# Token sums in four parts behind the evacuations of a chunk, and no modulation steps in that chunk

## The chip, the cores and the metric

The kernel runs on one core of one Trainium2 chip. The metric is device time in microseconds (us) of one execution. TensorE (PE) multiplies, VectorE (DVE), ScalarE (ACT) and GpSimd (POOL) do the element-wise work, and SyncE (SP) issues most of the transfers. Each engine takes its instructions from its own queue, in order.

## The reference

What is computed is a two-layer transformer on 512 latent tokens and 256 context tokens with a width of 1024. In each layer a half feed-forward step (SwiGLU, inner width 2816), a token mixer (neighbourhood attention in layer 0, windowed attention in layer 1) and a second half feed-forward step follow each other. Each of them is modulated by vectors that a product of the conditioning vector with a large matrix gives (`wmod`), and is closed by a layer norm:

```python
def swiglu(u, w_in, w_out):
    a, v = jnp.split(u @ w_in, 2, axis=-1)
    return (jax.nn.silu(a) * v) @ w_out

def ffn_sublayer(h, shift, scale, gate, w_in, w_out, g, b):
    y = swiglu(modulate(h, shift, scale), w_in, w_out)
    return layer_norm(ALPHA * h + FFN_RES * gate * y, g, b)
```

All of it is float32.

## The kernel before

**Layout.** Activations lie feature-major: eight tiles of 128 features by 768 tokens. A float32 value is kept as the sum of a high and a low part in TensorE's fp32r format, so `uh[d]` and `ul[d]` together are the modulated input of a step, and each product is three matmuls (lines L146, L147, L148: high by high, low by high, high by low). `z[d]` is the residual.

**Four feed-forward calls.** They are named 0a, 0b, 1a and 1b (layer, first or second half step) and all run through `ffn`. The inner width is cut into 11 chunks of two 128-row tiles. A *plain* chunk computes its a and v products for group a (512 tokens; 256 in 1b) and for group b (256 tokens), in the order (a, tile 0), (b, 0), (a, 1), (b, 1). One such step is an `av`: 48 matmuls, then DVE multiplies v by silu(a) in place (`pv`, L451), ACT copies the high part (`gh`, L452) and DVE subtracts to get the low part (`gl`, L453). After the four of them 16 *downs* follow (`pd`, eight output tiles for each group), and DVE adds each to the residual (`z`, L427). The downs of such a chunk, and the products of the chunks after it, take their PSUM banks from a ring of six.

**Seven products.** The first chunks are plain: three in 0a (chunks 0, 1, 2), two in 0b, 1a and 1b (chunks 0, 1). This number is `s0`. From chunk `s0` to chunk 8 each tile is computed by a Strassen-Winograd scheme on halves of the tokens and quarters of the weights: seven products p0 to p6 in place of eight (`seven`), whose evacuations DVE and ACT do (L565, L569). A tile's seven are followed by the next, and between the two of one chunk the downs of the chunk before run. POOL makes the sums of weight quarters (`S`, L536) and low parts of weights (`wl`, L104).

**Token sums.** The scheme needs sums of the token halves: `x1`, `x2` and `x3`, each for four pairs of feature tiles j. For one j these are 5 DVE operations and 3 POOL operations (L485), 3 ACT copies to the high parts and 3 DVE subtractions to the low parts (`T`, L507), all on 128x384 elements (128x256 in 1b). `sums()` writes them down at the start of chunk `s0 - 1`, with eight transfers per call that save the halves to be overwritten later. `fourth()` makes the fourth sum in place after that chunk (two POOL, one ACT and two DVE operations per j, L517 to L521); only product 6 needs it. Products 3, 2 and 5 need x1, x2 and x3.

**Modulation steps.** The modulation vectors of later steps are computed in the background on DVE. One *step* is a multiply-and-reduce `jk` of 128x512 elements (L198) followed by a 128x1 read of the accumulator. Its weights come in 256 KB loads that SP issues (L195) into two buffers `wt` and a spare tile `zspare`, so that at most three loads are out at a time. A load serves two steps where the vectors of the latent and the context tokens are both wanted ("two streams"), one step otherwise. `tick()` issues steps by a counter: `weight` (L601) gives each chunk its share and `each` (L602) scales the shares so that all steps of the call fit. 0a, 0b and 1a have such steps, 1b has none.

**What sets the order.** The order written in the code is a wish. A scheduler plays all instructions through a timeline and puts each engine's queue in the order in which they would start there; on the chip a queue is then worked off strictly in order. `behind(x, y)` (L308) adds a constraint: x stays behind y on the same engine. `last[0]` is the latest multiply, accumulate or product evacuation. Steps are issued `behind` it. In the kernel before, the token sums have no such constraint, so the scheduler puts them as early as their inputs exist.

Of the kernel before, what the change touches and what calls it, by code (L numbers as in the profile page):

```python
# [8 lines left out]
F32 = mybir.dt.float32  # L9
F32R = mybir.dt.float32r  # L10
# [3 lines left out]
ALU = mybir.AluOpType  # L14
# [4 lines left out]
P = 128  # L19
# [7 lines left out]
NCH = NF // 2  # L27
# [11 lines left out]
def hybrid_kernel(ctx: ExitStack, tc: tile.TileContext, h0, cc, crow, wmod, wmodt, bmod, lnp, wst,  # L39
                  rpbp, nmask, sinks, ropec, rmat, ident, wmask, out):  # L40
    nc = tc.nc
# [5 lines left out]
    dp = ctx.enter_context(tc.tile_pool(name="dp", bufs=1, space=DRAM))  # L47
# [5 lines left out]
    def t2(nm, tag="t2"):  # L53
        return tp.tile([P, 512], F32, tag=tag, name=nm, bufs={"t2": 6, "ln": 2, "sl": 2}[tag])
# [25 lines left out]
    uh = [rp.tile([P, NT], F32R, name=f"uh{d}") for d in range(DT)]  # L80
    ul = [rp.tile([P, NT], F32R, name=f"ul{d}") for d in range(DT)]
# [104 lines left out]
    bg, last, last_exp, wtq = [], [None], [None], [0]  # L186
# [244 lines left out]
    def ffn(nm, groups, gt, mid, post, units=(), opened={}, head=None, apart=None):  # L431
# [40 lines left out]
        n2 = nb * P  # L472

        def half(t, h):

            return t[:, 0:nb * 256].rearrange("p (a s b) -> p s a b", s=2, b=P)[:, h]

        def as_half(t):
            return t.rearrange("p (a b) -> p a b", b=P)

        ts = [[[None, None] for _ in range(4)] for _ in range(3)]

        def op(eng, out, a, b, o):
            a, b = [half(y[0], y[1]).bitcast(F32) if isinstance(y, tuple) else as_half(y) for y in (a, b)]
            eng.tensor_tensor(out=as_half(out), in0=a, in1=b, op=o)  # L485

        def sums():


            saved = dp.tile([2, 4, P, n2], F32, name=f"sv{nm}")  # L490
            for j in range(4):
                for x, t in enumerate((uh, ul)):
                    nc.sync.dma_start(saved[x, j].rearrange("p (a b) -> p a b", b=P), half(t[j], 1).bitcast(F32))
                x1, x2, x3 = [t2(f"x{nm}_{j}_{i}")[:, 0:n2] for i in range(3)]
                k = j + 4
                op(nc.vector, x1, (uh[j], 1), (uh[j], 0), ALU.subtract)
                op(nc.vector, x1, x1, (ul[j], 1), ALU.add)
                op(nc.vector, x1, x1, (ul[j], 0), ALU.subtract)
                op(nc.gpsimd, x3, (uh[k], 1), (uh[j], 1), ALU.subtract)
                op(nc.gpsimd, x3, x3, (ul[k], 1), ALU.add)  # L500
                op(nc.gpsimd, x3, x3, (ul[j], 1), ALU.subtract)
                op(nc.vector, x2, (uh[k], 1), x1, ALU.subtract)
                op(nc.vector, x2, x2, (ul[k], 1), ALU.add)
                for i, x in enumerate((x1, x2, x3)):
                    hi, lo = [ph["T"].tile([P, 384], F32R, tag=f"T{i}{j}{y}", name=f"T{nm}_{i}_{j}{y}", bufs=1)[:, 0:n2] for y in "hl"]
                    nc.scalar.copy(hi, x)
                    nc.vector.tensor_tensor(out=lo, in0=x, in1=hi.bitcast(F32), op=ALU.subtract)  # L507
                    ts[i][j] = [as_half(hi), as_half(lo)]
            return saved

        def fourth():

# [83 lines left out]
        if mid is not None:  # L596
            mid()
        gts.append(gt())
        late_downs = []
        s0 = 3 if opened else 2  # L600
        weight = [0] + [1.6] * (s0 - 1) + [1.0] * (NCH - 2 - s0)  # L601
        each = sum(n + 1 for n, _ in bg) / (sum(weight) - 0.1)  # L602
        for ci in list(range(NCH)) + [("r", NCH - 2)]:
            r = isinstance(ci, tuple)
            if not r and 0 < ci < NCH - 2:
                phase("T")
                pace[0] = each * weight[ci] / (4 if ci < s0 else 14)
                if ci == s0 - 1:
                    saved = sums()
            if not r and s0 <= ci < NCH - 2:  # L610
                gs = [[gp.tile([P, NT], F32R, tag="gs", name=f"g{x}{nm}_{ci}_{i}", bufs=6) for x in "hl"] for i in range(2)]

# [29 lines left out]
            def avs(*todo):  # L642
                for g, i in todo:
                    av(w[i], f"{cn}_{i}", g, *gs[i], opened.get((i, g)) if ci == 0 else None, 4 if late else 0)
                    if not r and 0 < ci < s0:
                        tick()

            def dn(g):
                down(w[2], cn, gs, g, not r and 0 < ci < NCH - 2)

            a, b = groups
# [654 lines left out]
```

## Time and profile before

| | |
|---|---|
| median of three runs | 2864.95 us (2863.02 to 2868.26) |
| the profiled execution | 2872.14 us, its span 2870.4 us |
| mean granted TensorE clock | 0.977 |
| PE busy | 2723.7 us (95% of the span) |
| DVE busy | 1857.1 us (65%) |
| ACT busy | 1211.9 us (42%) |
| POOL busy | 1687.2 us (59%) |
| modulation steps in all | 416, of 0.68 us each |
| idle time of DVE before steps, waiting for a load | 62.1 us (`wt`) and 12.3 us (`zspare`) |

The profile is of one execution. Tile names in it have lost their numbers: `pd0b` is any down of call 0b, `x0b` any token sum of it, `p60a` a product 6 of 0a. A row of the view by windows gives, for a stretch of time, each engine's busy time and number of instructions, and then the clock that TensorE was granted as a share of full speed. A row of waits gives an engine's operation, what it waited for, the total in us, the number of waits and the longest.

In the times of the span, chunk 0 of 0a ends near 130 us and its chunk-2 downs run from 195.6 to 212.6; the seven products of 0a run to 490. 0b's chunk 0 is near 1086 to 1122, its chunk-1 downs are at 1140.9 to 1169.2, its products run to 1480. 1a's chunk 0 is near 1640, its chunk-1 downs are at 1700.4 to 1717.4, its products run to 2040. 1b's chunks 0 and 1 lie at 2500 to 2550.

### The profile page before, as it was taken

The numbers are of one execution on the slowest core, as the hardware profiler recorded it, in microseconds if no ns is written. First come the engines' busy times: TensorE is split into PE (matmuls) and PEld (weight loads), VectorE is DVE, ScalarE is ACT, GpSimd is POOL, SyncE is SP. The second block draws the span as 40 slices with busy tenths as digits, with TensorE's granted clock in tenths as the row PEclk, the third lists the DMA queues.
The fourth block names the chain that finished last, engine by engine and source line by source line (L and its number), as shares of the span: only waits on it lengthen the run. The fifth ranks groups of instructions, "written<-read, shape, count | busy, mean of one in ns | idle before, by whom it ended". The sixth has DMA issues, their size and how long they took to land.

```text
span 2870.4 us, 48094 instructions
## 1 busy us (share of the span) xinstructions
PE 2723.7 (95%) x17122; PEld 2444.4 (85%) x17122; DVE 1857.1 (65%) x4122; ACT 1211.9 (42%) x2496; POOL 1687.2 (59%) x1488
## 2 busy tenths in 40 slices
PE   8999999999999979999999899999998999899997
PEld 5789999888888878899998789899886777788897
DVE  3597776385545687766554886666457667787745
ACT  4223433266455453333433424333336655444443
POOL 4547674475433565776744777666456545577763
PEclk9999999999999989999999999999999999999998
DMA  8465556232211222445452345656431111235462
GB/s 299 126 189 161 157 141 162 78 85 83 65 56 51 65 60 88 114 125 136 118 139 74 93 119 140 175 153 181 133 95 46 51 38 45 60 89 129 122 180 67
DMA packets 285872, 322.16 MB, mean 112 GB/s; under 512 B 28480, under 2 KB 174016, under 8 KB 284608
## 3 DMA queue, kind: packets, MB, share of 16 engines
q1 hardware_dynamic: 269792, 290.63, 34.2%
q0 software_dynamic: 15552, 28.32, 5.9%
q8 instruction: 135, 2.21, 0.3%
q14 instruction: 105, 0.86, 0.1%
q10 hardware_dynamic: 288, 0.14, 0.0%
HBM read 311.14 MB, written 12.25 MB: 113 GB/s over the span
## 4 chain that ended last, share of the span: by engine, by line
PE 73%; DVE 14%; DMA 5%; issue 3%; ACT 2%; POOL 2%; SPq 0%; DVEq 0%; POOLq 0%; ACTq 0%
DMA wt<-in_wmodt_dram 2%; PE pd0b L146 2%; PE pd0b L147 2%; PE pd0b L148 2%; DVE jk L198 2%; PE pd1a L146 2%; PE pd1a L147 2%; PE pd1a L148 2%; DMA wr<-in_wst_dram 1%; DVE z L427 1%; PE pd0a L146 1%; PE wo L753 1%; PE pd0a L147 1%; PE pd0a L148 1%; PE o L753 1%
## 5 line engine op out<-in xcount | busy, mean ns | idle before, releaser
L104 POOL TENSOR_TENSOR wl<-wr,wh 128x512 fp32r<-128x512 f32 x308 | 406.4, 1335 | 293.2 <-ACT wh L102 261.5
L104 POOL TENSOR_TENSOR wl_s<-S,wh_s 128x512 fp32r<-128x512 f32 x202 | 269.2, 1368 | 52.8 <-ACT wh_s L102 49.5
L102 ACT CAST wh<-wr 128x512 fp32r<-128x512 f32 x308 | 186.8, 620 | 225.7 <-DMA wr<-in_wst_dram 54.5
L102 ACT CAST wh_s<-S 128x512 fp32r<-128x512 f32 x216 | 131.6, 620 | 335.7 <-POOL S L536 79.6
L536 POOL TENSOR_TENSOR S<-wr,wr 128x512 f32<-128x512 f32 x108 | 147.6, 1367 | 180.2 <-DMA wr<-in_wst_dram 172.0
L198 DVE CUSTOM_DVE_ANT_0 jk<-wt,cb 128x512 f32<-128x512 f32 x278 | 185.2, 680 | 63.7 <-DMA wt<-in_wmodt_dram 62.1
L104 POOL TENSOR_TENSOR wl_a<-wr,wh_a 128x512 fp32r<-128x512 f32 x120 | 159.6, 1383 | 26.7 <-ACT wh_a L102 17.5
L102 ACT CAST wh_a<-wr 128x512 fp32r<-128x512 f32 x162 | 100.5, 621 | 134.1 <-PE pd1b L147 18.1
L427 DVE SCALAR_TENSOR_TENSOR z<-pd0b,gt,z 128x256 f32<-128x256 f32 (+1 forms) x176 | 102.3, 602 | 62.7 <-PE pd0b L148 62.5
L427 DVE SCALAR_TENSOR_TENSOR z<-pd1a,gt,z 128x512 f32<-128x512 f32 (+1 forms) x168 | 99.0, 620 | 39.2 <-PE pd1a L148 39.0
L427 DVE SCALAR_TENSOR_TENSOR z<-pd0a,gt,z 128x512 f32<-128x512 f32 (+1 forms) x168 | 98.1, 620 | 31.9 <-PE pd0a L148 31.5
L760 POOL TENSOR_SCALAR p<-p,l 128x512 f32<-128x512 f32 x64 | 44.5, 696 | 118.9 <-DVE l L858 110.5
L305 POOL TENSOR_SCALAR z<-z,ag_None,ab_None 128x256 f32<-128x256 f32 (+1 forms) x78 | 73.0, 942 | 47.6 <-DVE uh L291 38.7
L198 DVE CUSTOM_DVE_ANT_0 jk<-zspare,cb 128x512 f32<-128x512 f32 x138 | 92.5, 680 | 12.3 <-DMA zspare<-in_wmodt_dram 12.3
L760 POOL TENSOR_SCALAR pw<-pw,l 128x512 f32<-128x512 f32 (+1 forms) x64 | 41.0, 642 | 68.2 <-DVE l L1047 27.7
L536 POOL TENSOR_TENSOR S<-S,wr 128x512 f32<-128x512 f32 x54 | 77.2, 1429 | 2.9 <-DVE x1b L519 0.4
L536 POOL TENSOR_TENSOR S<-wr,S 128x512 f32<-128x512 f32 x54 | 76.4, 1414 | 3.1 <-PE pv0a L148 0.5
L857 ACT ACTIVATE p<-s,m 128x512 f32<-128x512 f32 x64 | 44.0, 688 | 76.2 <-DVE m L855 71.2
L287 ACT ACTIVATE ufl<-z,bi_None,sc_None 128x256 f32<-128x256 f32 (+1 forms) x86 | 54.5, 654 | 37.2 <-DVE z L406 36.9
L427 DVE SCALAR_TENSOR_TENSOR z<-pd1b,gt,z 128x512 f32<-128x512 f32 (+1 forms) x98 | 56.3, 609 | 13.1 <-PE pd1b L148 13.1
L292 DVE TENSOR_TENSOR ul<-ufl,uh 128x256 fp32r<-128x256 f32 (+1 forms) x88 | 61.7, 711 | 1.0 <-ACT uh L289 0.7
L146 PE MATMUL vn<-wh,uh 128*128 128x256 f32 x192 | 54.9, 286 | 2.4 <-DVE nl L716 1.8
(1445 smaller groups left out, 10757.9 us busy)
## 6 DMA issues: line engine op xcount, KB each, us to landing
wr<-in_wst_dram SPq DMA_DIRECT2D x524, 256.0 KB
wt<-in_wmodt_dram SPq DMA_DIRECT2D x160, 256.0 KB
zspare<-in_wmodt_dram SPq DMA_DIRECT2D x80, 256.0 KB
wr_0b<-in_wst_dram SPq DMA_DIRECT2D x42, 256.0 KB
wr_1b<-in_wst_dram SPq DMA_DIRECT2D x42, 256.0 KB
wr_2b<-in_wst_dram SPq DMA_DIRECT2D x42, 256.0 KB
wr_3b<-in_wst_dram SPq DMA_DIRECT2D x42, 256.0 KB
wm<-in_wmod_dram SPq DMA_DIRECT2D x8, 1024.0 KB
```

The source lines that it names most:

```text
L102: nc.scalar.copy(hi[:], src[:])
L104: eng.tensor_tensor(out=lo[:], in0=src[:], in1=hi[:].bitcast(F32), op=ALU.subtract)
L146: nc.tensor.matmul(ps, a[0], b[0], start=first, stop=False)
L147: nc.tensor.matmul(ps, a[0], b[1], start=False, stop=False)
L148: nc.tensor.matmul(ps, a[1], b[0], start=False, stop=last)
L198: x = nc.vector.tensor_tensor_reduce(out=junk[:], in0=w[:], in1=cb[st], scale=1.0, scalar=0.0, op0=ALU.mult, op1=ALU.add, accum_out=acc[:, ...
L292: return hi, nc.vector.tensor_tensor(out=lo, in0=uv, in1=uo.bitcast(F32), op=ALU.subtract)
L305: nc.gpsimd.tensor_scalar(out=zs, in0=zs, scalar1=prm[2][:, d:d + 1], scalar2=prm[3][:, d:d + 1], op0=ALU.mult, op1=ALU.add)
L427: last[0] = nc.vector.scalar_tensor_tensor(out=zt(d, c0, c1), in0=pd, scalar=gt[:, d, st:st + 1], in1=zt(d, c0, c1), op0=ALU.mult, op1=ALU ...
L536: nc.gpsimd.tensor_tensor(out=t[:], in0=a[:], in1=b[:], op=o)
L753: nc.tensor.matmul(po[64 * h:64 * h + 64, :], t[h][0], t[h][1], start=i == 0, stop=i == len(terms) - 1)
L760: nc.gpsimd.tensor_scalar(out=p, in0=p, scalar1=r, scalar2=0.0, op0=ALU.mult, op1=ALU.add)
```

## The change

`sums()` is split. The saving transfers become `save()`, still issued at the start of chunk `s0 - 1`. The rest becomes `sums(j)`, called once behind each of the four `av` steps of that chunk, one j at a time, and each DVE operation of it is kept `behind` the latest multiply or accumulate. POOL's operations are written at the same places but have no constraint that binds them to DVE's. `fourth()` stays where it is. The weight of chunk `s0 - 1` becomes 0, so that no modulation steps are issued in it: in 0a the weights go from 0, 1.6, 1.6 and six of 1 to 0, 1.6, 0 and six of 1; in 0b, 1a and 1b from 0, 1.6 and seven of 1 to 0, 0 and seven of 1. As `each` scales by the sum of the weights, the other chunks get more. No operation is added or removed.

```diff
         def op(eng, out, a, b, o):
             a, b = [half(y[0], y[1]).bitcast(F32) if isinstance(y, tuple) else as_half(y) for y in (a, b)]
-            eng.tensor_tensor(out=as_half(out), in0=a, in1=b, op=o)
-
-        def sums():
-
-
-            saved = dp.tile([2, 4, P, n2], F32, name=f"sv{nm}")
+            behind(eng.tensor_tensor(out=as_half(out), in0=a, in1=b, op=o), last[0])
+
+        def save(saved):
+
             for j in range(4):
                 for x, t in enumerate((uh, ul)):
                     nc.sync.dma_start(saved[x, j].rearrange("p (a b) -> p a b", b=P), half(t[j], 1).bitcast(F32))
...
+        def sums(j):
+
+            x1, x2, x3 = [t2(f"x{nm}_{j}_{i}")[:, 0:n2] for i in range(3)]
...
+            for i, x in enumerate((x1, x2, x3)):
...
+                nc.scalar.copy(hi, x)
+                behind(nc.vector.tensor_tensor(out=lo, in0=x, in1=hi.bitcast(F32), op=ALU.subtract), last[0])
+                ts[i][j] = [as_half(hi), as_half(lo)]
...
-        weight = [0] + [1.6] * (s0 - 1) + [1.0] * (NCH - 2 - s0)
+        weight = [0] + [1.6] * (s0 - 2) + [0] + [1.0] * (NCH - 2 - s0)
...
                 if ci == s0 - 1:
-                    saved = sums()
+                    saved = dp.tile([2, 4, P, n2], F32, name=f"sv{nm}")
+                    save(saved)
...
+                    if not r and ci == s0 - 1:
+                        sums(js.pop(0))
```

How the change moves the queues is shown at three places on DVE. The first is the end of chunk 0 of call 0a; the rows with a minus stand there before, those with a plus in the changed kernel (`pv0a_0_512` and `gl0a_0` are the multiply and the low part of group b, `x0a` token sums, `T0a` their low parts).

```order
-L485 TENSOR_TENSOR x0a_0_1372<-uh_101 128x384
-L485 TENSOR_TENSOR x0a_0_1372<-x0a_0_1372,ul_109 128x384 x2
-L485 TENSOR_TENSOR x0a_1_1373<-uh_105,x0a_0_1372 128x384
-L485 TENSOR_TENSOR x0a_0_1397<-uh_102 128x384
-L451 TENSOR_TENSOR pv0a_0_512_1005<-pv0a_0_512_1005,sl0a_0_512_1030 128x256
-L485 TENSOR_TENSOR x0a_1_1373<-x0a_1_1373,ul_113 128x384
-L507 TENSOR_TENSOR T0a_0l<-x0a_0_1372,T0a_0h 128x384
-L485 TENSOR_TENSOR x0a_0_1397<-x0a_0_1397,ul_110 128x384
-L453 TENSOR_TENSOR gl0a_0_891<-pv0a_0_512_1005,gh0a_0_890 128x256
+L451 TENSOR_TENSOR pv0a_0_512_1011<-pv0a_0_512_1011,sl0a_0_512_1036 128x256
+L453 TENSOR_TENSOR gl0a_0_891<-pv0a_0_512_1011,gh0a_0_890 128x256
```

Seven token sums stood among the evacuations of chunk 0; now none does, and they come two chunks later.

The second place is the end of chunk 1 of call 0b, where the last `av` (b, 1) is evacuated and the downs begin. Before:

```order
L451 TENSOR_TENSOR pv0b_1_512_12587<-pv0b_1_512_12587,sl0b_1_512_12612 128x256
L485 TENSOR_TENSOR x0b_1_12247<-x0b_1_12247,ul_116 128x384
L519 TENSOR_TENSOR x0b_4_12765<-x0b_4_12765,x0b_5_12767 128x384
L198 ISA jk_7_0_0_12560,ga_0_11335<-wt_7_0_12558,cb_0_0_0_12402 128x512
L198 ISA ga_0_11335 128x1
L521 TENSOR_TENSOR ul_109<-x0b_4_12758,uh_101 128x3x128
L198 ISA jk_7_0_1_12617,ga_0_11335<-wt_7_0_12558,cb_0_0_1_12406 128x512
L198 ISA ga_0_11335 128x1
L453 TENSOR_TENSOR gl0b_1_12344<-pv0b_1_512_12587,gh0b_1_12343 128x256
L427 SCALAR_TENSOR_TENSOR z_92<-pd0b_0_0_12630,gt_8_11336,z_92 128x512
```

and in the changed kernel:

```order
L451 TENSOR_TENSOR pv0b_1_512_12526<-pv0b_1_512_12526,sl0b_1_512_12551 128x256
L485 TENSOR_TENSOR x0b_0_12556<-uh_104 128x384
L508 TENSOR_TENSOR T0b_2l<-x0b_1_12479,T0b_2h 128x384
L453 TENSOR_TENSOR gl0b_1_12252<-pv0b_1_512_12526,gh0b_1_12251 128x256
L485 TENSOR_TENSOR x0b_0_12556<-x0b_0_12556,ul_112 128x384
L427 SCALAR_TENSOR_TENSOR z_92<-pd0b_0_0_12579,gt_8_11336,z_92 128x512
L485 TENSOR_TENSOR x0b_0_12556<-x0b_0_12556,ul_112 128x384
L427 SCALAR_TENSOR_TENSOR z_93<-pd0b_0_1_12587,gt_8_11336,z_93 128x512
L485 TENSOR_TENSOR x0b_1_12557<-uh_108,x0b_0_12556 128x384
L427 SCALAR_TENSOR_TENSOR z_94<-pd0b_0_2_12595,gt_8_11336,z_94 128x512
L508 TENSOR_TENSOR T0b_3l<-x0b_0_12556,T0b_3h 128x384
L485 TENSOR_TENSOR x0b_1_12557<-x0b_1_12557,ul_116 128x384
```

The steps between multiply and low part are gone, and the last part of the token sums stands between the first accumulates. Behind these rows there follow two more `T`, the other accumulates and the eight operations of `fourth()`. In 0a and 1a the end of the chunk reads alike.

The third place is in a seven of call 1a (chunk 7, first tile, one stream): the evacuations from product 4 to the first low part. Before:

```order
L565 TENSOR_TENSOR y1a_0_1_21050<-p41a_0_21124,y11a_0_21052 128x384
L198 ISA jk_51_1_0_21141,ga_40_17472<-wt_51_1_21139,cb_40_1_0_20895 128x512
L198 ISA ga_40_17472 128x1
L565 TENSOR_TENSOR y01a_0_21051<-p51a_0_21143,y01a_0_21051 128x384
L565 TENSOR_TENSOR p51a_0_21143<-p51a_0_21143,y11a_0_21052 128x384
L565 TENSOR_TENSOR p51a_0_21143<-p51a_0_21143,y1a_0_1_21050 128x384
L565 TENSOR_TENSOR p61a_0_21165<-y01a_0_21051,p61a_0_21165 128x384
L565 TENSOR_TENSOR gl1a_0_21002<-p51a_0_21143,gh1a_0_21001 128x3x128
```

and in the changed kernel:

```order
L565 TENSOR_TENSOR y1a_0_1_21028<-p41a_0_21106,y11a_0_21030 128x384
L198 ISA jk_43_1_0_21083,ga_40_17472<-wt_43_1_21081,cb_40_1_0_20973 128x512
L198 ISA ga_40_17472 128x1
L565 TENSOR_TENSOR y01a_0_21029<-p51a_0_21125,y01a_0_21029 128x384
L565 TENSOR_TENSOR p51a_0_21125<-p51a_0_21125,y11a_0_21030 128x384
L198 ISA jk_44_1_0_21086,ga_40_17472<-zspare,cb_40_1_0_20973 128x512
L198 ISA ga_40_17472 128x1
L198 ISA jk_45_1_0_21104,ga_40_17472<-wt_45_1_21102,cb_40_1_0_20973 128x512
L198 ISA ga_40_17472 128x1
L565 TENSOR_TENSOR p51a_0_21125<-p51a_0_21125,y1a_0_1_21028 128x384
L565 TENSOR_TENSOR p61a_0_21150<-y01a_0_21029,p61a_0_21150 128x384
```

Where one step and its load stood among these evacuations, there are now three.

More of the change, by code (lines that the diff above doesn't have):

```diff
@@ L493, in sums @@
                     nc.sync.dma_start(saved[x, j].rearrange("p (a b) -> p a b", b=P), half(t[j], 1).bitcast(F32))
[L494 to L509, printed above, removed]
+        def sums(j):
+            x1, x2, x3 = [t2(f"x{nm}_{j}_{i}")[:, 0:n2] for i in range(3)]
+            k = j + 4
+            op(nc.vector, x1, (uh[j], 1), (uh[j], 0), ALU.subtract)
+            op(nc.vector, x1, x1, (ul[j], 1), ALU.add)
+            op(nc.vector, x1, x1, (ul[j], 0), ALU.subtract)
+            op(nc.gpsimd, x3, (uh[k], 1), (uh[j], 1), ALU.subtract)
+            op(nc.gpsimd, x3, x3, (ul[k], 1), ALU.add)
+            op(nc.gpsimd, x3, x3, (ul[j], 1), ALU.subtract)
+            op(nc.vector, x2, (uh[k], 1), x1, ALU.subtract)
+            op(nc.vector, x2, x2, (ul[k], 1), ALU.add)
+            for i, x in enumerate((x1, x2, x3)):
+                hi, lo = [ph["T"].tile([P, 384], F32R, tag=f"T{i}{j}{y}", name=f"T{nm}_{i}_{j}{y}", bufs=1)[:, 0:n2] for y in "hl"]
+                nc.scalar.copy(hi, x)
+                behind(nc.vector.tensor_tensor(out=lo, in0=x, in1=hi.bitcast(F32), op=ALU.subtract), last[0])
+                ts[i][j] = [as_half(hi), as_half(lo)]
         def fourth():
@@ L598, in ffn @@
         gts.append(gt())
-        late_downs = []
+        late_downs, js = [], [0, 1, 2, 3]
         s0 = 3 if opened else 2
-        weight = [0] + [1.6] * (s0 - 1) + [1.0] * (NCH - 2 - s0)
+        weight = [0] + [1.6] * (s0 - 2) + [0] + [1.0] * (NCH - 2 - s0)
         each = sum(n + 1 for n, _ in bg) / (sum(weight) - 0.1)
```

## The prediction

> **What bounds the kernel now.** I read the page first, then TensorE's waits in the four places where token sums are made, then the same places by windows. The first line of the page:
>
> ```profile
> PE 2723.7 (95%) x17122; PEld 2444.4 (85%) x17122; DVE 1857.1 (65%) x4122; ACT 1211.9 (42%) x2496; POOL 1687.2 (59%) x1488
> ```
>
> TensorE sets the end. The change touches no matmul, so it can only win or lose where TensorE waits for DVE. These are its waits (engine, what waits, for what: total us, times, longest) at the end of chunk 0 and start of chunk 1 of 0a (111 to 151 us), then in 0b (1086 to 1171), 1a (1638 to 1668) and 1b (2524 to 2541):
>
> ```profile
> PE pd0a L146 <- DVE z L427: 6.7, 5, 2.4
> ...
> PE pd0b L146 <- DVE gl0b L453: 3.4, 1, 3.4
> PE pd0b L146 <- ACT gh0b L452: 2.1, 1, 2.1
> PE pa0b L147 <- DVE ul L292: 0.9, 1, 0.9
> PE pv0b L146 <- DVE gl0b L453: 0.9, 1, 0.9
> ...
> PE pv1a L146 <- DVE gl1a L453: 2.7, 1, 2.7
> PE pd1a L146 <- DVE z L427: 1.8, 2, 1.2
> PE pa1a L147 <- DVE ul L292: 1.3, 1, 1.3
> ...
> PE pd1b L146 <- DVE zspare L427: 3.6, 1, 3.6
> PE pv1b L146 <- DVE gl1b L453: 1.4, 1, 1.4
> PE pd1b L146 <- DVE z L427: 0.9, 1, 0.9
> ```
>
> The view by windows adds the granted clock, the third column from the end:
>
> ```profile
> core 0: us, PE busy (x) PEld busy (x) DVE busy (x) ACT busy (x) POOL busy (x), PEclk, DMA share, GB/s
> 111.00:151.00 40.00, 33.30 (x166) 28.49 (x165) 37.34 (x67) 11.61 (x23) 31.60 (x25) 0.87 0.63 180
> 1086.00:1094.00 8.00, 6.21 (x37) 5.80 (x37) 7.96 (x12) 1.00 (x2) 6.42 (x6) 0.79 0.29 78
> 1140.90:1169.20 28.30, 22.16 (x100) 18.12 (x99) 28.30 (x57) 8.60 (x18) 20.47 (x16) 0.82 0.25 76
> 1638.00:1667.00 29.00, 23.13 (x107) 18.57 (x106) 28.93 (x36) 7.70 (x17) 27.05 (x21) 0.94 0.29 82
> 1700.40:1717.40 17.00, 17.00 (x99) 14.89 (x98) 16.32 (x32) 3.78 (x9) 15.19 (x12) 1.00 0.41 122
> 2525.00:2541.00 16.00, 10.21 (x70) 9.51 (x70) 14.90 (x29) 6.41 (x16) 13.35 (x13) 0.88 0.09 24
> 2541.00:2560.00 19.00, 19.00 (x151) 19.00 (x151) 15.02 (x27) 8.01 (x15) 13.71 (x10) 0.92 0.30 87
> ```
>
> DVE is busy 93 to 100% of these windows while it is at 65% over the span, and the clock falls below 1 behind the waits. The chunk-1 downs of 0b take 28.3 us; the same downs in 1a take 17.0.
>
> **What there is to win: 43.5 us.** Waits plus clock loss (length times one less the clock). 0a: 6.7 + 40 x 0.13 = 11.9. 0b, chunk 0: 0.9 + 0.9 + 8 x 0.21 = 3.5; its downs: 28.3 - 17.0 = 11.3. 1a: 5.8 + 29 x 0.06 = 7.5. 1b: 5.9 + 16 x 0.12 + 19 x 0.08 = 9.3. In all these places token sums stand among the evacuations (first and second place of the order), and the change takes them out of chunk 0 altogether. I take the whole 43.5 as gone there.
>
> A rule bears on the clock part. The Trainium skill, "TensorE: Matmul & The Clock Gate", section "HAM oscillation — how this bites in real kernels", says in short that only idle gaps above some 3.4 us bring the half clock. Here 0a has 0.87 with no wait above 2.4 us, so the rows do not follow it. By the rule some 17 of the 43.5 would not be winnable and the sum below would be 17 lower, about 2882; as the rows contradict it, I give that no chance of its own.
>
> **What comes back behind the last av: -29.** The sums are not made cheaper, only moved. Three of the four parts fall into the products of chunk `s0 - 1`, where DVE now has no steps: free. The fourth part cannot start before the last multiply and then stands, with all of `fourth()`, between the accumulates. Durations from DVE's groups in 0b between 1086 and 1171 us (busy, mean ns):
>
> ```profile
> L427 DVE SCALAR_TENSOR_TENSOR z<-pd0b,gt,z 128x256 f32<-128x256 f32 x26 | 12.1, 478 | 15.0 <-PE pd0b L148 14.9
> L485 DVE TENSOR_TENSOR x0b<-x0b,ul 128x384 f32<-128x384 f32 x10 | 10.2, 1028 | 0.0
> L427 DVE SCALAR_TENSOR_TENSOR z<-pd0b,gt,z 128x512 f32<-128x512 f32 x8 | 5.6, 739 | 0.0
> L521 DVE TENSOR_TENSOR ul<-x0b,uh 128x384 fp32r<-128x384 f32 x4 | 4.1, 1014 | 0.0
> L507 DVE TENSOR_TENSOR T0b_1l<-x0b,T0b_1h 128x384 fp32r<-128x384 f32 x3 | 4.0, 1348 | 0.0
> L519 DVE TENSOR_TENSOR x0b<-x0b,x0b 128x384 f32<-128x384 f32 x4 | 3.9, 981 | 0.0
> ```
>
> and, over all of a call, the spread of a sum (min/median/max ns):
>
> ```profile
> L485 DVE TENSOR_TENSOR x0b<-x0b,ul x12: 544/780/1684, 1075.7 to 1150.9; 128x384 f32<-128x384 f32 x12
> ```
>
> With 1.0 us for each sum, 0.74 for a wide accumulate and 0.48 for a narrow one, I go down the changed order from the end of the last av (0; multiply done by about 1, which is my estimate): z0 done at 5.2, z1 6.9, z2 8.6, z3 12.4, z4 15.1, z5 15.8, z6 18.5, z7 20.2, then the narrow ones 21.7, 22.2, 24.7. TensorE takes 17.0 us for sixteen downs, so about 1.4 for a wide and 0.7 for a narrow one, and the ring of six lets it run six ahead: down 9 needs z3, down 10 z4 and so on. It waits 0.3 at z3, 2.0 at z4, 2.0 at z6, 1.0 at z7, 0.8 and 1.6 at the narrow ones, in sum 7.7. Three calls give 23; 1b, with shorter operations and shorter downs, I put at 6. Together -29. Ends: with 0.55 us for each sum (the minimum) there is no wait at all; with 1.35 (the `T0b_1l` row) the sixteen sums and `fourth()` operations cost 5.6 more in each of three calls and 4 in 1b, -50. I take 1.0 because three of the four rows say so. POOL's parts add no work, and if its third x3 came late, a `T` would hold DVE's queue: this is in the upper end. The eight saving transfers stay where they were: 0.
>
> The spread of 544 to 1684 ns has a reading in the Trainium skill, "SBUF — State Buffer", section "SBUF: two separate sides": a DVE operation with two SBUF inputs and a GpSimd operation that reads SBUF exclude each other for a whole instruction. By that rule every sum beside POOL's work would go to the long end, and the tail would cost the -50.
>
> **What denser steps cost: -15.** The steps taken out go to chunk 1 of 0a, where DVE has just been relieved of sums (I put that at 0: its 1.6 shares rise from 33 to 40 steps, 7 x 0.68 = 4.8 us, against 32 sum operations of 0.55 to 1.0 us that leave chunks 0 and 1; without that cover it would be up to 4.8), and into the sevens. The rows of 0a (215 to 490 us) and of 1a (1722 to 2040):
>
> ```profile
> L198 DVE CUSTOM_DVE_ANT_0 jk<-wt,cb 128x512 f32<-128x512 f32 x83 | 54.8, 680 | 20.0 <-DMA wt<-in_wmodt_dram 20.0
> L198 DVE CUSTOM_DVE_ANT_0 jk<-zspare,cb 128x512 f32<-128x512 f32 x42 | 28.1, 680 | 5.7 <-DMA zspare<-in_wmodt_dram 5.7
> ...
> L198 DVE CUSTOM_DVE_ANT_0 jk<-wt,cb 128x512 f32<-128x512 f32 x66 | 44.7, 680 | 37.6 <-DMA wt<-in_wmodt_dram 36.8 <-ACT cb L211 0.7
> L198 DVE CUSTOM_DVE_ANT_0 jk<-zspare,cb 128x512 f32<-128x512 f32 x34 | 23.0, 679 | 4.5 <-DMA zspare<-in_wmodt_dram 4.5
> ```
>
> In 0a that is 125 steps in six chunks, 20.8 for each; the sum of weights less 0.1 goes from 9.1 to 7.5, so 25.3: 2.2 more for each seven. In 1a 100 steps in seven chunks, factor 8.5 / 6.9: 1.65 more. Whether TensorE feels it depends on how late DVE is when the downs begin. Two chunks of 1a, from one product 6 over seven and downs to the next, and the last low part of the earlier product 6 in each:
>
> ```profile
> 1953.30:1984.60 31.30, 31.30 (x182) 29.32 (x182) 20.15 (x46) 9.06 (x16) 25.09 (x20) 1.00 0.48 144
> 1999.20:2033.20 34.00, 31.83 (x181) 29.05 (x180) 23.21 (x56) 12.56 (x23) 22.04 (x19) 1.00 0.66 177
> ...
> 1959.70 0.55 DVE L565 TENSOR_TENSOR gl1a<-p61a,gh1a 128x384 fp32r<-128x384 f32 x1
> 2008.97 0.55 DVE L565 TENSOR_TENSOR gl1a<-p61a,gh1a 128x384 fp32r<-128x384 f32 x1
> ```
>
> Done 7.0 us late it costs nothing; 10.3 us late it costs 2.7, 0.8 for each us beyond 7. TensorE's waits in the sevens of 0a (two rows) and 1a (two) say that both stand at that point already, while 0b's (last row) is far from it:
>
> ```profile
> PE pd0a L146 <- DVE gl0a L565: 3.2, 2, 2.3
> PE pd0a L146 <- DVE z L427: 1.2, 3, 0.8
> ...
> PE pd1a L146 <- DVE gl1a L565: 6.4, 3, 3.3
> PE pd1a L146 <- DVE z L427: 1.1, 2, 0.8
> ...
> PE pd0b L146 <- DVE gl0b L565: 0.3, 1, 0.3
> ```
>
> A step costs 0.68 us plus its share of DVE's waits for loads: 25.7 / 125 = 0.21 in 0a, 42.1 / 100 = 0.42 in 1a. So 0a: 2.2 x 0.89 x 0.8 x 5 downs = 7.8; 1a: 1.65 x 1.1 x 0.8 x 6 = 8.7. Without any further wait for loads it would be 6 + 5.4 = 11. I take -15. Ends: 0, if DVE's idle time before the evacuations takes up the steps; -32, if the second seven of a chunk hands its delay to the first of the next, which has no downs in between. 0b: 0, its cover is the 0.3 us row.
>
> **Sum.** 43.5 - 29 - 15 = about 0 against the profiled 2872.14 us, whose span is 2870.4. The median of the runs shown is 7.2 below that execution, so the forecast is 2865. The measurement can tell about 0.2%, 5.7 us either way, from no change.
>
> **Rivals.** *Clean gain.* Sums at their median of 0.78 us: the tail costs 4.2 in each of three calls and 4 in 1b, 17; and DVE absorbs two thirds of the density, -5. 43.5 - 17 - 5 = +21.5: 2844. For it: three parts of four lie on a DVE without steps, and POOL is not reading all the time. Against: the order puts 16 sum operations in a stretch of 17 us that also has 16 accumulates.
>
> *The sevens become bound by DVE.* From about 10 us late at the downs a chunk loses what is added: -32 in place of -15, so 43.5 - 29 - 32 = -17.5: 2882, slower. For it: the 2.7 us chunk above and the 36.8 us that DVE waited for `wt` loads in 1a. Against: 0a's waits come to only 4.4 in six chunks.
>
> *The stall moves instead of going.* With sums at 1.35 us the tail takes -50 and eats the whole 43.5; density then leaves 43.5 - 50 - 15 = -21.5: 2886. That would also be the case in which the change does not do what it says: the sums are still in DVE's way, only at the downs. For it: 0b's tail before, with 100% DVE; against: 1a's tail of 17.0 us with 16.32 of DVE busy and no wait.
>
> **Chances.** Forecast (2857 to 2873) 0.36, clean gain 0.32, bound sevens 0.22, moved stall 0.10. Faster: 0.30 of the clean gain and 0.06 of the forecast, 0.36. Slower: 0.21 + 0.10 and 0.04 of the forecast, 0.35. The same: 0.29. The range takes in the clean gain at 2844 and the moved stall at 2886 with a little beyond each: 2842 to 2890.
>
> **What would show it.** Right: no waits of TensorE and a clock of 1.00 between chunks 0 and 1 of all four calls; waits `pd <- DVE z` of 5 to 9 us per call in the downs of the last plain chunk; downs of 0b near 24 us where they took 28.3; intervals over the downs in 0a and 1a longer by 1 to 2 us, 0b's unchanged. Wrong: those downs at 17 us (clean gain); intervals longer by 3 us and more (bound sevens); or waits left in chunk 0, which would mean that the sums were not their cause.

## The result, and the profile after

The changed kernel takes 2881.6 us (median; 2880.4 to 2883.9) against 2866.6 us for the kernel before, measured beside it: a ratio of 1.0054 with a 95% interval of 1.0032 to 1.0077. It is slower, by 9 to 22 us. The profiled execution took 2880.37 us, its span is 2878.6 us. One run of all that follow lay far outside, at 10708 us (one of ten of the change in 0b alone); medians and ratios leave it out.

The two profiles differ by 8.2 us in the span and the medians by 15.0. The profiled execution of the kernel before was itself 5.5 us above its median; one of its chunks in 1a took 37.2 us at a clock of 0.91 (from 1853.6 us) where its neighbours take 31 to 34. So a difference of 5 us in one call of one profile is not yet a finding, and below each is held against the other runs.

The four calls by windows, from the first a product to the last down of each (0a, 0b, 1a, 1b), before:

```profile
16.50:609.10 592.60, 574.97 (x3191) 505.56 (x3192) 383.94 (x870) 208.20 (x376) 342.25 (x281) 0.99 0.54 156
1037.70:1605.80 568.10, 549.79 (x3209) 512.31 (x3210) 358.47 (x759) 218.06 (x409) 356.65 (x300) 0.97 0.40 107
1597.80:2162.80 565.00, 543.23 (x3074) 498.82 (x3072) 374.14 (x774) 213.01 (x386) 364.59 (x294) 0.98 0.49 135
2468.90:2847.80 378.90, 367.11 (x2687) 349.88 (x2688) 257.01 (x483) 175.28 (x362) 259.00 (x215) 0.98 0.45 117
```

and after:

```profile
16.60:619.60 603.00, 573.68 (x3191) 505.07 (x3192) 390.04 (x870) 207.92 (x377) 340.51 (x281) 0.98 0.53 153
1049.30:1607.40 558.10, 541.58 (x3209) 506.00 (x3210) 355.67 (x759) 218.17 (x409) 355.33 (x300) 0.99 0.40 109
1599.40:2166.50 567.10, 542.36 (x3074) 498.36 (x3073) 369.54 (x776) 212.56 (x386) 360.28 (x294) 0.98 0.48 135
2472.90:2854.70 381.80, 367.71 (x2687) 347.54 (x2688) 253.90 (x483) 175.90 (x362) 257.76 (x215) 0.99 0.45 116
```

0a lost 10.4 us, 0b won 10.0, 1a lost 2.1, 1b lost 2.9. The waits of TensorE that answer to the four groups shown before, in the plain chunks of 0a (103 to 161 us), 0b (1096 to 1174), 1a (1640 to 1723) and 1b (2524 to 2553):

```profile
PE pd0a L146 <- DVE z L427: 10.1, 1, 10.1
...
PE pd0b L146 <- DVE z L427: 4.0, 5, 1.3
PE p00b L146 <- DVE z L427: 1.4, 1, 1.4
...
PE pd1a L146 <- DVE z L427: 4.0, 4, 2.3
PE p01a L146 <- DVE z L427: 1.4, 1, 1.4
PE pd1a L146 <- DVE gl1a L453: 1.3, 1, 1.3
PE pd1a L147 <- DVE gl1a L453: 0.3, 1, 0.3
...
PE pd1b L146 <- DVE zspare L427: 2.0, 1, 2.0
```

In 0b and 1a all the waits of before are gone, and in 1b one is left, shortened from 3.6 to 2.0 us. What is there now lies in the downs of the last plain chunk and is, in 0b and 1a, made mostly of short waits for z. In 0a five waits of 6.7 us in sum have become one of 10.1 us, and the clock fell behind it. The windows of that stretch and of the downs behind the last av of 0a and of 1a:

```profile
103.00:161.00 58.00, 47.92 (x267) 41.65 (x268) 33.28 (x81) 9.70 (x17) 14.69 (x13) 0.88 0.60 169
196.00:219.20 23.20, 18.83 (x91) 15.60 (x92) 23.16 (x32) 5.75 (x12) 19.82 (x16) 0.93 0.00 1
1700.00:1720.00 20.00, 13.32 (x71) 11.34 (x71) 20.00 (x28) 5.07 (x10) 18.20 (x15) 0.91 0.00 1
```

In the first, DVE is busy for 33 of 58 us: it is not overloaded, it waits. DVE's timeline there, and SyncE's of the same time (start, us, engine, line, what; the idle time before it in brackets), and below the last dots two rows of the kernel before:

```profile
128.39 0.68 DVE L198 CUSTOM_DVE_ANT_0 jk<-zspare,cb 128x512 f32<-128x512 f32 x1
...
141.35 0.69 DVE L198 CUSTOM_DVE_ANT_0 jk<-wt,cb 128x512 f32<-128x512 f32 x1 [12.27 <-DMA wt<-in_wmodt_dram]
...
142.57 0.48 DVE L427 SCALAR_TENSOR_TENSOR z<-pd0a,gt,z 128x256 f32<-128x256 f32 x1
...
114.18 15.41 SPq L782 DMA_DIRECT2D yd<-xd  x16
130.21 0.69 SPq L94 DMA_DIRECT2D wr<-in_wst_dram  x1
131.67 0.33 SPq L195 DMA_DIRECT2D wt<-in_wmodt_dram  x1
...
117.76 15.03 SPq L779 DMA_DIRECT2D yd<-xd  x16
147.27 0.69 DVE L198 CUSTOM_DVE_ANT_0 jk<-wt,cb 128x512 f32<-128x512 f32 x1 [0.66 <-DMA wt<-in_wmodt_dram]
```

The three loads that may be out at a time had been used up by 128.99 us. The fourth stood on SyncE's queue behind sixteen transfers `yd` (the bias tables of the first mixer, L782), which held the queue for 15.4 us; it was issued at 131.67 and used at 141.35. So the transfers delayed it twice: the first of the three buffers was free at 125.9, 5.8 us before the issue, and the load then took 9.7 us to arrive, where the same load took 4.0 us in the run below that has the transfers elsewhere (issued at 127.19, used at 131.20). The step that needed it stood ahead of the accumulate `z` on DVE, the accumulate held a PSUM bank, and TensorE waited. In the kernel before the same sixteen transfers held SyncE from 117.76 us for 15.03 us, but DVE was making token sums then and its first step of that chunk that needed a new load came at 147.27, with 0.66 us of waiting. So the sums, by standing early, had covered the tables; the experiments with the tables below test that.

### The profile page after: what moved, and what is told of

Its sections match the earlier page's. It is cut to its first block, busy times and chain, and to the rows that moved or that the text cites. A ratio compares the mean times of both kernels' runs of the same rounds, so it can differ in the third digit from the quotient of the medians.

```text
span 2878.6 us, 48112 instructions
## 1 busy us (share of the span) xinstructions
PE 2716.6 (94%) x17122; PEld 2437.7 (85%) x17122; DVE 1852.7 (64%) x4122; ACT 1213.3 (42%) x2496; POOL 1678.4 (58%) x1488
## 4 chain that ended last, share of the span: by engine, by line
PE 71%; DVE 14%; DMA 6%; issue 3%; ACT 3%; POOL 2%; SPq 0%; DVEq 0%; POOLq 0%; ACTq 0%
PE pd0b L147 2%; PE pd0b L148 2%; PE pd0b L146 2%; DVE z L427 2%; DMA wt<-in_wmodt_dram 2%; DMA wr<-in_wst_dram 2%; PE pd1a L146 2%; PE pd1a L148 2%; PE pd1a L147 2%; PE pd0a L146 1%; PE wo L756 1%; PE pd0a L147 1%; PE pd0a L148 1%; DVE jk L198 1%; DMA zspare<-in_wmodt_dram 1%
## 5 line engine op out<-in xcount | busy, mean ns | idle before, releaser
L287 ACT ACTIVATE ufl<-z,bi_None,sc_None 128x256 f32<-128x256 f32 (+1 forms) x86 | 54.4, 656 | 35.7 <-DVE z L406 35.3
L146 PE MATMUL pd0a<-gh0a,wh 128*128 128x512 f32 (+1 forms) x144 | 51.1, 367 | 15.9 <-DVE z L427 14.0
```

The costliest lines, as they stand in the source:

```text
L146: nc.tensor.matmul(ps, a[0], b[0], start=first, stop=False)
L287: nc.scalar.activation(uf[:, :n], zs, AF.Identity, scale=s1, bias=s2)
```

## The experiments

Each ratio is to the kernel before, run on the same chip, with its 95% interval. "Plain" is the time of a call from its first a product to its first product 0.

**One part of the change alone.** The sums in four parts with the weights as before:

```diff
-        weight = [0] + [1.6] * (s0 - 2) + [0] + [1.0] * (NCH - 2 - s0)
+        weight = [0] + [1.6] * (s0 - 1) + [1.0] * (NCH - 2 - s0)
```

> The token sums in four parts as in the change, but the weights of the steps as before (1.6 for the chunk with the sums too). Density theory (the prediction's own terms: 43.5 won in front, 29 lost in the downs, 15 lost to denser steps): without the 15 this is about 14 us faster than before, some 2852. Queue theory (the loss is a wait of the first steps of call 0a for loads that stand on SyncE's queue behind the sixteen table transfers, which the token sums used to cover): the sums have left that place here too, so the wait of about 10 us stays, and the time is within 5 us of before; 0a keeps a TensorE wait near 143 us of the span.

It took 2900.7 us, 1.0135 (1.0096 to 1.0174): slower than the whole change by some 19 us. Neither theory had that. The wait in 0a is there (9.1 us at 141.7), but the larger part is new: in 0a (222 to 500 us), 0b (1172 to 1200) and 1a (1730 to 1760) TensorE waits at product 2 of the first seven,

```profile
PE p20a L146 <- ACT wh_s L102: 10.8, 1, 10.8
...
PE p20b L146 <- ACT wh_s L102: 7.4, 1, 7.4
...
PE p21a L146 <- ACT wh_s L102: 9.5, 1, 9.5
```

for a weight sum that POOL had not made. POOL's timeline in 1a shows why:

```profile
1725.22 1.01 POOL L518 TENSOR_TENSOR x1a<-T1a_1h,uh 128x384 f32<-128x384 f32 x1 [4.24 <-DVE T1a_3l L508]
1728.22 1.02 POOL L518 TENSOR_TENSOR x1a<-T1a_1l,ul 128x384 f32<-128x384 f32 x1 [1.99 <-DVE T1a_2l L508]
1733.63 1.02 POOL L518 TENSOR_TENSOR x1a<-T1a_2h,uh 128x384 f32<-128x384 f32 x1 [4.39 <-DVE T1a_3l L508]
...
1741.63 1.58 POOL L536 TENSOR_TENSOR S<-wr,wr 128x512 f32<-128x512 f32 x1
```

POOL's share of `fourth()` waits for `T` on DVE, DVE does steps and accumulates first, and behind the waiting instruction on POOL's queue stand the weight sums `S`. In the changed kernel POOL waits 1.5 us in that place and its first `S` starts at 1714.21, in time. So here the two parts of the change belong together: with the steps left in that chunk, the sums came too late at its end.

The weights of the change with the sums as before:

```diff
-        weight = [0] + [1.6] * (s0 - 1) + [1.0] * (NCH - 2 - s0)
+        weight = [0] + [1.6] * (s0 - 2) + [0] + [1.0] * (NCH - 2 - s0)
```

> The weights of the change (no steps in the chunk with the sums) with the token sums as before. Density theory: 15 us slower than before in the sevens of 0a and 1a, less what 0b's downs win (up to 8 us), so about 2870 to 2882. Queue theory: the sums still cover the table transfers, the wait near 143 us of the span is not there; the time lies within 5 us of before and most of 0b's gain is seen.

It took 2872.2 us, 1.0029 (1.0008 to 1.0050): 6.3 us above the kernel beside it, within what density theory gave and just outside the 5 us of queue theory, though its interval allows both. Its 0b took 560.6 us, nearly as short as in the changed kernel: what 0b won came mostly from the weights. 0a has no wait of 10 us, its plain part takes 194.1 us. The remaining step to the changed kernel's 1.0054 comes with the sums, though the two intervals overlap.

**The tables elsewhere.** In the changed kernel the tables were written at chunk 9 in place of chunk 1, and, for comparison, in the kernel before as well:

```diff
-            if mid is not None and ci == 1:
+            if mid is not None and ci == NCH - 2:
                 bias_tables()
```

> The change with the table transfers of the first mixer (eight xd, sixteen yd) written at chunk 9 of call 0a in place of chunk 1. Queue theory: the 12.3 us wait of VectorE for a load and TensorE's 10.1 us wait behind it go, 9 to 11 us faster than the changed kernel, about 2871. Density theory: within 3 us of the changed kernel, 2881, since the sevens are as dense as there.

> The kernel before with the same move of the table transfers, the comparison for the run above. Queue theory: the sums cover the transfers there, so the move is worth 0 to 4 us. If it is worth as much here as in the changed kernel, the transfers are a cost of their own that has nothing to do with the change.

The changed kernel with late tables took 2884.3 us, 1.0067 (1.0042 to 1.0092); the kernel before with late tables 2877.8, 1.0051 (1.0032 to 1.0070). In the first the wait at 143 us is gone (0.9 us is left), DVE waits 3.7 us for loads there in place of 12.3, and 0a's plain part falls from 202.4 to 195.1 us. But in both TensorE now waits near 530 us, in the one 11.7 and in the other 11.2 us:

```profile
PE pa0a L146 <- ACT wh L102: 11.7, 1, 11.7
...
PE pa0a L146 <- ACT wh L102: 11.2, 1, 11.2
```

The transfers hold SyncE for 15.45 us there too, and now it is weights (`wr`) that stand behind them. The cause of the wait is confirmed, but the expected times were missed: moved, the same 15 us of queue hurt something else. Against each other, the two kernels with late tables differ by 6.5 us, and 0a's plain part is 194.7 us in the one and 195.1 in the other; with the tables at chunk 1 the change cost 15.0 us, and 6.4 in that part. (By their intervals the two with late tables cannot be told apart.)

So they were spread, three in each chunk of sevens:

```diff
-        for h in range(NH):
-            nc.sync.dma_start(yd[h], xd[h]...)
+    def spread_tables(part):
+        for h in range(3 * part, min(NH, 3 * part + 3)):
+            behind(nc.sync.dma_start(yd[h], xd[h]...), loaded[0])
...
+                    if i == 0 and mid is not None:
+                        spread_tables(ci - s0)
```

> The change with the sixteen yd transfers of the tables written three at a time, one group in each chunk of sevens of call 0a, so that they never hold SyncE's queue for more than about 3 us; the xd transfers stay. Queue theory (the 10.1 us wait of TensorE in chunk 1 of 0a is the steps' loads behind these transfers, and in the run with the tables at chunk 9 the same transfers held back weights instead, 11.8 us near 533 us): neither wait is there, 8 to 11 us faster than the changed kernel, about 2872. Rival (0a loses by the density of its steps alone): the wait near 143 us goes, but the time stays within 3 us of 2881.

2882.9 us, 1.0064 (1.0049 to 1.0079). 0a's plain part took 191.9 us, 10.5 less than in the changed kernel and the shortest of all; but its sevens gave that back: 0a took 604.8 us in all, against 603.0. TensorE's waits in them (215 to 490 us) are 9.6 us for z and 5.0 for low parts, 14.6, against 7.2 in the changed kernel:

```profile
PE pd0a L146 <- DVE z L427: 9.6, 4, 4.0
PE pd0a L146 <- DVE gl0a L565: 5.0, 1, 5.0
```

DVE waited 35.4 us for the steps' loads in the same stretch, against 24.7 in the changed kernel, so the transfers seem to delay the loads there too; that was not tried apart. By its time this run came out as the rival had it, and not as queue theory had it.

And from ScalarE's queue, at the old place:

```diff
-            nc.sync.dma_start(yd[h], xd[h]...)
+            nc.scalar.dma_start(yd[h], xd[h]...)
```

> The change with the sixteen yd transfers issued from ScalarE's queue in place of SyncE's, at the same place. Queue theory: the steps' loads of chunk 1 are issued at once, VectorE's 12.3 us wait and TensorE's 10.1 us wait near 143 us go, and nothing is put into the sevens: 7 to 10 us faster than the changed kernel, about 2873, less what ScalarE's evacuations lose while it issues (up to 10 us if the issue takes as long there). If the load itself is slow, and not its issue late, the wait stays.

2883.8 us, 1.0067 (1.0044 to 1.0090). The 12.3 us wait for the load is down to 3.9, but a new one of 6.4 us stands beside it: ScalarE, which makes the vectors `cb` that the steps multiply by, was issuing the transfers in its turn:

```profile
DVE jk L198 <- ACT cb L211: 6.4, 1, 6.4
DVE jk L198 <- DMA wt<-in_wmodt_dram: 3.9, 1, 3.9
```

What the transfers and the sums do to each other is seen best in one stretch of 0a, from TensorE's last product for the modulation vectors near 100 us (`gm`) to the end of the downs of chunk 1. Each profile has 298 or 299 matmuls in it:

| kernel | stretch, us | TensorE's waits in it, us | clock |
|---|---|---|---|
| before | 61.1 | 6.7 | 0.92 |
| before, tables late | 61.0 | 6.6 | 0.92 |
| the change | 62.3 | 10.1 | 0.89 |
| the change, tables late | 50.7 | 0.9 | 1.00 |
| the change, tables spread | 50.2 | 0.6 | 1.00 |
| the change, tables from ScalarE | 62.4 | 6.6 | 0.89 |

Either of the two, early sums or tables at chunk 1, is enough to hold this stretch at 61 to 62 us; only with both away is it 50 to 51. That is shown. It is not shown that this makes the whole kernel slower: two of the three ways to move the transfers freed 12 us here, the third none, and no kernel became faster: in those two, other waits grew.

**The last part out of the downs.** Parts behind the first, second and third av (one, one, two), then one, two, one, none behind the fourth:

```diff
-        late_downs, js = [], [0, 1, 2, 3]
+        late_downs, js = [], [[0], [1], [2, 3], []]
...
-                        sums(js.pop(0))
+                        for j in js.pop(0):
+                            sums(j)
```

> The change with the parts of the token sums behind the first (one), second (one) and third (two) av, none behind the fourth, so that only the fourth sum is left among the downs. The prediction's tail term says that the last part and the fourth sum together cost 7.7 us in each of 0a, 0b and 1a (5 to 6 us of TensorE waits for z were seen): without the last part the sixteen operations among the downs become eight, the waits in those downs fall to 0 to 2 us per call, and the time by 8 to 15 us, to about 2866 to 2873. If the fourth sum alone, or VectorE's accumulates, keep the ring of banks waiting, the time stays at 2881.

> The change with one part of the token sums behind the first av, two behind the second, one behind the third, none behind the fourth. The run with one, one and two showed that two parts behind the third av, a stretch of only 5.8 us, are themselves too much for VectorE there (10 us slower than the change). Here two parts stand before the long av of 11 us. If VectorE's work in the short stretches sets the waits: TensorE's waits in those downs fall from 5 to 6 us per call to 2 to 3, the time by 5 to 9 us, about 2875. If the fourth sum sets them, as POOL makes it from the last T: no change, 2881, or worse.

They took 2891.8 us, 1.0095 (1.0077 to 1.0112), and 2893.5 us, 1.0104 (1.0082 to 1.0125): some 10 us slower than the change, both expectations missed. The waits in the downs of 1a (1700 to 1735 us) in the two runs:

```profile
PE pd1a L146 <- DVE z L427: 5.6, 4, 3.4
PE pd1a L146 <- ACT gh1a L452: 0.6, 1, 0.6
PE pd1a L147 <- DVE gl1a L453: 0.5, 1, 0.5
...
PE pd1a L146 <- ACT gh1a L452: 5.0, 1, 5.0
PE pd1a L146 <- DVE z L427: 1.7, 3, 0.6
PE pd1a L147 <- DVE gl1a L453: 1.6, 1, 1.6
```

They are as large as before, 6.7 and 8.3 us against the 7.0 of the changed kernel shown above, and 1a's plain part grew from 120.4 to 125.2 and 123.1 us. With the sums ahead, an av itself is evacuated late. In the first of the two runs the multiply of the last av starts at 1708.45 us, 8.8 after the downs have begun (1699.68); in the second it is the multiply of the third av:

```profile
1704.55 1.36 DVE L508 TENSOR_TENSOR T1a_2l<-x1a,T1a_2h 128x384 fp32r<-128x384 f32 x1
1705.84 1.34 DVE L485 TENSOR_TENSOR x1a<-x1a,ul 128x384 f32<-128x384 f32 x1
1707.11 1.35 DVE L508 TENSOR_TENSOR T1a_1l<-x1a,T1a_1h 128x384 fp32r<-128x384 f32 x1
1708.38 0.55 DVE L508 TENSOR_TENSOR T1a_2l<-x1a,T1a_2h 128x384 fp32r<-128x384 f32 x1
1708.85 0.69 DVE L451 TENSOR_TENSOR pv1a<-pv1a,sl1a 128x512 f32<-128x512 f32 x1
```

DVE is busy for 24.00 of the 24 us from 1698 in the changed kernel, and for 28.93 of 29 and 39.86 of 40 in these (29 from 1700, 40 from 1690). That fits the view that its work there in sum sets the waits, and not which of it stands last; no run had less of that work.

**The calls one by one.** The change in one call or three, the others as before:

```diff
-        weight = [0] + [1.6] * (s0 - 2) + [0] + [1.0] * (NCH - 2 - s0)
+        weight = [0] + [1.6] * (s0 - 2) + [0 if nm in ("0b",) else 1.6] + [1.0] * (NCH - 2 - s0)
...
                     save(saved)
+                    if nm not in ("0b",):
+                        for j in range(4):
+                            sums(j)
...
-                    if not r and ci == s0 - 1:
+                    if not r and ci == s0 - 1 and nm in ("0b",):
                         sums(js.pop(0))
```

with `("0b",)`, the same with parts one, one, two, none, then `("0a",)` and `("0b", "1a", "1b")`; the order constraint of the sums is dropped in the calls left out.

> Both parts of the change in call 0b alone; 0a, 1a and 1b as before. By the segments of the profiles 0b won 10 us (568.1 to 558.1) while 0a lost 10 and 1b 3: so 8 to 10 us faster than before, about 2857. If the calls were coupled (a delay in one paid back in another), it would be within 5 us of before.

> As the run above, with the parts of 0b behind the first (one), second (one) and third (two) av. If the tail term holds in 0b (4.8 us of TensorE waits among its downs and the first product in the changed kernel), another 3 to 5 us less than that run, about 2853; if the fourth sum is what holds the downs, no difference.

> Both parts of the change in call 0a alone; 0b, 1a and 1b as before. If 0a is where the loss is (10 us of TensorE waiting behind the steps' loads in chunk 1, some 6 us from denser steps in its sevens, less the waits that the sums made before): 10 to 15 us slower than before, 2875 to 2880. If the loss of the change is spread over all calls: within 5 us of before.

> Both parts of the change in 0b, 1a and 1b, 0a as before; the counterpart of the run above. If the loss is 0a's: 2 to 8 us above before at most (denser steps in 1a against 0b's gain), about 2868. If it is spread: 8 to 12 us above before.

| the change in | median us | ratio | 0a | 0b | 1a | 1b |
|---|---|---|---|---|---|---|
| none (before) | 2866.6 | 1 | 592.6 | 568.1 | 565.0 | 378.9 |
| none, tables late | 2877.8 | 1.0051 (1.0032 to 1.0070) | 601.5 | 563.9 | 557.9 | 383.2 |
| 0b | 2868.2 | 1.0014 (1.0003 to 1.0026) | 587.3 | 561.9 | 569.1 | 385.8 |
| 0b, parts 1, 1, 2, 0 | 2865.9 | 1.0009 (0.9999 to 1.0018) | 590.7 | 559.3 | 566.1 | 378.7 |
| 0a | 2893.6 | 1.0096 (1.0074 to 1.0118) | 602.4 | 564.4 | 577.6 | 379.8 |
| 0b, 1a, 1b | 2874.2 | 1.0026 (1.0008 to 1.0043) | 590.8 | 559.7 | 574.5 | 384.7 |
| all | 2881.6 | 1.0054 (1.0032 to 1.0077) | 603.0 | 558.1 | 567.1 | 381.8 |

(The last four columns are the calls of the profiled execution in us, between first a product and last down.) 0a takes 602 to 603 us in the two rows that have the change in it, and 587 to 593 where neither the change nor the late tables are: its loss is there each time, and by the medians the change without 0a is some 7 us faster than with it (the intervals overlap). The times do not settle where the loss is, though. The change without 0a lies 9.4 us above the kernel before beside it, where 2 to 8 was expected if the loss is 0a's and 8 to 12 if it is spread. 0a alone should have cost 10 to 15 us and cost 29 (against 2864.8 beside it); 12.6 of that is 1a, as follows. The two together come to 38 us where the whole change costs 15, so the calls do not simply add up. With the change in 0b that call takes 558 to 562 us, without it 564 to 568: some 5 us won, not the 10 of one profile. And a call whose code is the same does not keep its time: 1a with the code of before took 557.9, 565.0, 566.1, 569.1 and 577.6. Between the first two of these not one row of DVE's queue differs. In the last, the scheduler had also put 1a's queues in another order, though nothing in 1a was edited, and TensorE's four waits for low parts in its sevens came to 13.3 us:

```profile
PE pd1a L146 <- DVE gl1a L565: 13.3, 4, 4.9
```

So the expectation for 0b alone (8 to 10 us faster) failed: that run is not faster than before. The 0b-alone run with parts one, one, two is the fastest of the variants and level with the kernel before; the 2853 expected of it was missed. No variant beat the kernel before.

## Why the prediction was right or wrong

The time, 2881.6 us, lies in the range, and not at the forecast of 2865: the change is slower by more than the 0.2% that was called the limit. The range ran from 0.8% faster to 0.9% slower, so it says little that it held. By the steps:

- **"I take the whole 43.5 as gone there."** Right in 0b, 1a and 1b, where no wait of before is left in front. Wrong in 0a, and this is the step that failed. The size was right: without sums and tables the stretch of the table above falls by 10.4 to 10.9 us, and 11.9 was put. But in the changed kernel it grew by 1.2, as one wait of 10.1 us came where five of 6.7 went. The step asked what the sums were delaying, and not what they were covering: it never named what the steps, now first on DVE, would wait for, and SyncE's queue in that stretch was not read. It has the sixteen transfers in the trace of before. Its error is 13 us.
- **Waits plus clock loss.** The sum counts twice where the two fall together. For the changed kernel it would give 10.1 + 58 x 0.12 = 17.1 us at this place; but of the 13.6 us that the clock stood at 0.50 there (135.1 to 148.7), 8 lie inside the wait itself (133.0 to 143.1).
- **The place.** The first excerpt of the order was said to be the end of chunk 0 of 0a. The rows drop part of the names; `pv0a_0_512` there is chunk 1, first tile. The downs of chunk 0 run among those of chunk 1's products, so the argument held, but the words were wrong, and the sums come one chunk later, not two. DVE's 93 to 100% does not hold for the last of the windows shown, where it is busy for 15.02 of 19 us.
- **"What comes back behind the last av: -29."** Sized about right: the operations of the last part and of the fourth sum that stand between 1701 and 1722 us in 1a take 0.96 us in the mean, 1.0 was taken. The long end throughout, which the prediction drew from the Trainium skill ("SBUF — State Buffer", section "SBUF: two separate sides"), was not reached: they took 0.54 to 1.64 us. From the first of these downs to the first product 0, 0a takes 23.0 us (16.9 before), 0b 23.8 (30.2 before; 24 was named as a sign of being right) and 1a 26.7 (17.7 before). Against the 17.0 that sixteen downs take without a wait that is 6.0, 6.8 and 9.7, each put at 7.7. 1b, put at 6, shows 2.0 us of waits and is 2.5 us shorter there than before. The reason behind it, that the last part is what delays the accumulates, did not hold in the form given: taken out of the downs, it delayed the last av instead.
- **"What denser steps cost: -15."** The direction was right, the mechanism was not what the rows show. For 0a the four intervals from the downs of chunk 3 to those of chunk 7 took 183.1 to 186.0 us in six profiles with the old weights in 0a and 186.0 to 192.8 in seven with the new (the run with spread tables left out): 5.8 us more in the mean, against 7.8 predicted. But the cost is not spread over them, as a chunk bound by denser steps would have it. The first of the four took 45.9 us in each of the six and 47.6 to 54.4 in the seven; the other three together took 138.2 and 138.6 in the mean. In that first interval each of the seven has a step that waits 4.7 to 6.6 us for `cb`, where the steps change from one half of the vectors to the other; in the changed kernel TensorE then waits 5.3 us for z. None of the six has it there. So this looks like one more wait for an input that the new place of the steps laid open; why `cb` came late was not tried. For 1a the five like intervals took 231.8 to 250.4 with the old weights and 238.9 to 242.5 with the new: 1.4 us more in the mean, which the spread of the old hides. The 8.7 predicted there was not seen.
- **Not foreseen in 1b.** It won 3.9 us in its plain part (80.4 to 76.5), as the sum 9.3 - 6 said, and lost 4.4 in its first two sevens and the downs behind (42.5 to 46.9), on late weights (`wh_s`, `wl_s`, and a `wl` load). That is no chance of one profile: the stretch took 46.5 to 47.4 us in the six profiles with the change's sums in 1b and 40.8 to 42.6 in the six with the old. Which of the changed orders made these weights late was not tried.

By measured lengths the sum reads as follows. The plain parts, where 43.5 - 29 = 14.5 us were to be won, won 7.6: 0a -6.4 (with 2.6 us won before 100 us, a start that took 81.8 to 86.6 us from run to run), 0b +10.1, 1a 0.0, 1b +3.9. Behind them 0a lost 4.0, 0b 0.1, 1a 2.1 and 1b 6.8, which is 13.0, near the 15 foreseen but not where it was foreseen. Outside the calls 2.8 were lost. That makes the 8.2 us by which the profiles differ. These are single profiles: by the other runs 0b won some 5 us. Most of the rest of the 15 between the medians is the profiled execution of before, 5.5 us slower than its median.

Of the rivals, *clean gain* is out. *Bound sevens* gave 2882, which is near by luck: its mechanism, a loss in each chunk, is not what 0a's intervals show. *The stall moves instead of going* is nearest in kind: but it had the stall move to the downs, and in 0a it moved to a wait for loads behind SyncE's queue. The argument against it, that 1a's downs had no wait before, did not hold: they have 7.0 us of waits now.

On the clock rule of the Trainium skill ("TensorE: Matmul & The Clock Gate", section "HAM oscillation — how this bites in real kernels"), which has the half clock only behind longer gaps, the trace after disagrees again: 0a's downs at 196 us ran at 0.93 and 1a's at 0.91 with no single wait above 2.4 us.

## What to carry to other kernels

Before work is moved out of an engine's way, ask what it is covering: read the queue that issues the loads of whatever comes next on that engine, for the stretch where it will now come, and see what stands in that queue. On in-order queues a background step that waits for a load is as hard a stop as any other, and everything behind it pays. When one edit moves work and another makes room for it, measure each alone; here the first alone cost 35 us where both together cost 15. And where a scheduler orders all queues at once, one profile of a call that was not edited is no control: 1a varied by some 20 us here, and by 7 between two profiles in which its queues had the same order.

## What the hardware showed beyond that

- The sixteen `yd` transfers held the queue that issued them for 15.0 to 15.5 us: on SyncE at chunk 1 before and after, on SyncE at chunk 9, and on ScalarE (4.6 us for six and 10.7 for ten). In the changed kernel the first ten went out some 0.7 us apart and the last six some 1.45 us apart. The next loads, of 256 KB, followed at 1.4 us each, although all but the first were themselves on the queue for only 0.33 us. So a long row of transfers slowed what was issued behind it, too. Three at a time, in the run with spread tables, none was on the queue for more than 0.77 us.
- The same program varies by 0.8%: the kernel before took 2853.4 to 2875.7 us in 22 runs on one chip. Its interval needs several runs, and one profile of it can be 5 us off.
